# An MLP's other engines in a written order: ACT, DVE, POOL and SyncE follow the products' places

## The chip, the cores and the metric

The kernel runs on one core of one Trainium2 chip. It is one launch that computes a whole decoder block; the time is device microseconds of that launch. The core has five instruction streams that matter here: TensorE (PE, with the weight loads shown apart as PEld), VectorE (DVE), ScalarE (ACT), GpSimd (POOL) and SyncE (SP), which in the kernel before issues every DMA. Each stream runs its instructions in the order in which the built program has them and waits on semaphores for the others.

## The reference

The block has an attention and a gating branch, whose merged output is projected and added to x; the change leaves them alone. What matters is the squared-ReLU MLP behind them, on 2048 tokens, width 1024, inner width 4096, in float32:

```python
h = _rmsnorm(x, norm_pre_mlp[layer])
a = jax.nn.relu(jnp.einsum('bsd,df->bsf', h, w_mlp_in[layer]))
y = jnp.einsum('bsf,fd->bsd', a * a, w_mlp_out[layer])
x = x + _rmsnorm(y, norm_post_mlp[layer])
```

## The kernel before

**Numbers.** Each float32 operand is split in a high part (hi, rounded to the matmul's fp32r type: an ACT copy, L70) and a low part (lo, the difference: a subtraction on DVE or POOL, L75). A product of two operands is three matmuls: hi x hi, hi x lo, lo x hi.

**Products.** Both matrix products of the MLP use a scheme with seven block products in place of eight. Sums and differences of blocks are formed ahead, and the products are added up in PSUM and behind it.

GEMM1 (h times w_mlp_in) works on two token halves, first half 1 and then half 0, and in each on 16 pairs q of inner blocks. A product (L918) is 12 matmuls of 128x512. Names: A11, A12, A22, S1 to S4 are weight-side operands (tags wh and wl), B11, B21, B22 and T1 to T4 are token-side operands (T2_first is T2 of the first half). Digits behind a name are half and q: S2_13 is S2 of half 1, q = 3, and w1r_131 is the second raw weight tile of half 1, q = 3. For each q:

- two raw tiles w1r (512 KB each, tag w1r, 5 buffers) are loaded by SP; POOL forms four sums from them (L899 to L902, sum_a), ACT and DVE split the results;
- A11 and A12 of a q that stands in an "ahead" zone are loaded alone (lone_a, tile ar, 256 KB), in a buffer of the tag "c" that the outputs s1, s2, s4 use too;
- outputs: products 6 and 7 are added to xs on DVE (u6, u7, L939), products 5/7, 4 and 3 end in an add (L942) and relu and square on ACT (L927, L928); product 3 ends the q with four POOL operations (L955, L957, L959, L961). SP stores the seven results to sd in DRAM.

`places` sets PE's order by a place for each product: the first LEAD = 4 q have products 1 and 2 ahead, then a chain of five products per q, then seven products per q in the middle, and the last three q are again ahead and chain. The second half follows in the same way. The first products (A11, A12 with B11, B21) run while the block before, `out_block`, still transposes the last tokens; that block makes the T operands and stores them to td (L821), from which load_t fetches them.

GEMM2 has 64 steps (8 groups of two q, 8 token blocks), each with seven products of 6 matmuls (L1197). A step needs two tiles s (448 KB each from sd, split on ACT and DVE) and the split sums of w_mlp_out (B11y, T2y and so on, lo on POOL, sums by sum_w2 in tiles w2r). DVE adds each product to the accumulator (L1204, L1207 the first time). In the last group each finished row block goes through `finish`: square with a row sum on ACT (L1176), gain on POOL (L1177), rstd_of on DVE (L94 to L103), result on DVE (L1182), store.

**Order.** Only PE follows an order written out by hand, the order of the code. The other engines' instructions are put in order by the scheduler, which may move them past one another. In the built program DMAs signal through eight completion counters used in turn, so an issue can have to wait until the DMA eight issues earlier has landed.

```python
for z2 in order[n:n + 14]:
    raw_need(*z2)
for z2 in order[n:n + 6]:
    need(*z2)
product(*z)
```

So before, raw tiles are asked for 14 products ahead, and all five splits of a q at once, 6 products ahead.

## Time and profile before

| | us |
|---|---|
| median of 3 runs | 2871.11 (2864.7 to 2871.95) |
| the profiled execution, its own time | 2863.28 |
| its span, first to last instruction | 2861.5 |
| PE busy in it | 2729.3 |
| GEMM1, first product of q's chain to last product | 1537.0 to 2183.9 |
| GEMM2, first to last product | 2183.9 to about 2849.7 |

A row of a window gives, for each engine, its busy time in that stretch, with the number of instructions; then the granted clock of PE, the busy share of the DMA engines and GB/s. A row of waits gives who waits for whom, in total, how often, and the longest. A row of the timeline gives start, length, engine, line, operation, out<-in, and in brackets how long the engine stood idle before it and what released it. Rows of SPq are DMA issues: the length is that of the issue with its waiting. Rows of groups give count, busy time, mean ns of one, and idle time before them.

### The profile page before, as it was taken

The page shows a single profiled execution, that of the slowest core. Times are in us where ns is not written, and L with a number is a line of the kernel's source. Part 1 is how long each engine was busy: PE and PEld are TensorE (multiplying, and loading weights), DVE is VectorE, ACT ScalarE, POOL GpSimd, SP SyncE. Part 2 cuts the span into 40 slices and gives each one's busy share as a digit, 9 for nine tenths or more (in the row PEclk, how much of TensorE's full clock was granted, in tenths as well). Part 3 has the DMA queues.
Part 4 walks back from the last instruction along what each step waited for, and adds up shares of the span by engine and source line. Part 5 has one row for each costly group of instructions (what it writes and reads, how often), then busy time and mean ns, then how long its engine had stood idle before and what let it go on. Part 6 is the DMA issues. An engine that isn't in the chain of part 4 may idle for free. (4 is left out here: it accounts for less than half of the span.)

```text
span 2861.5 us, 36328 instructions
## 1 busy us (share of the span) xinstructions
PE 2729.3 (95%) x13364; PEld 2287.1 (80%) x13364; DVE 1587.3 (55%) x2684; ACT 1039.1 (36%) x2039; POOL 1003.7 (35%) x703
## 2 busy tenths in 40 slices
...
GB/s 252 176 150 149 173 135 180 142 201 177 203 210 199 163 199 128 204 171 183 143 186 234 155 158 159 191 174 157 157 156 209 117 95 125 126 120 125 127 137 196
DMA packets 348370, 475.38 MB, mean 166 GB/s; under 512 B 19872, under 2 KB 222880, under 8 KB 348192
## 3 DMA queue, kind: packets, MB, share of 16 engines
...
## 5 line engine op out<-in xcount | busy, mean ns | idle before, releaser
L70 ACT ACTIVATE s<-s 128x896 fp32r<-128x896 f32 x128 | 121.9, 953 | 269.8 <-PE ya L1197 137.8
L918 PE MATMUL aa<-B,A 128*128 128x512 f32 x768 | 191.2, 400 | 11.6 <-ACT A L70 9.3
L1204 DVE TENSOR_TENSOR acc<-acc,ya 128x512 f32<-128x512 f32 x224 | 151.4, 683 | 80.2 <-PE ya L1197 79.7
L75 DVE TENSOR_TENSOR s<-s 128x896 fp32r<-128x896 f32 x128 | 169.5, 1326 | 44.6 <-ACT s L70 44.4
L918 PEld LDWEIGHTS aa<-B,A 128*128 128x128 f32 x768 | 146.5, 192 | 47.5 <-ACT A L70 10.5
L72 POOL TENSOR_SCALAR w_g<-w_g_r 128x1024 fp32r<-128x1024 f32 x32 | 34.2, 1068 | 411.2 <-PE g L87 384.8
L85 PE MATMUL x<-hT_a,wq 128*128 128x512 f32 x384 | 149.7, 390 | 0.0
L87 PE MATMUL x<-hT_a,wq 128*128 128x512 f32 x384 | 149.4, 389 | 0.0
L86 PE MATMUL x<-hT_a,wq 128*128 128x512 f32 x384 | 149.4, 389 | 0.0
L603 DVE TENSOR_REDUCE o<-po 128x256 f32<-128x512 f32 x48 | 33.2, 691 | 183.9 <-PE po L602 183.9
L918 PE MATMUL ab<-T_first,S 128*128 128x512 f32 x384 | 96.7, 402 | 24.2 <-ACT T_first L70 15.9
L70 ACT ACTIVATE hl<-r 128x512 fp32r<-128x512 f32 x48 | 30.4, 633 | 231.5 <-POOL r L248 86.7
L1197 PE MATMUL ya<-T2y,s 128*128 128x512 f32 x384 | 100.0, 396 | 13.8 <-ACT s L70 13.8
L75 POOL TENSOR_TENSOR T2y<-w2r,T2y 128x512 fp32r<-128x512 f32 x16 | 20.5, 1306 | 262.4 <-ACT T2y L70 262.4
L1197 PE MATMUL ya<-B11y,s 128*128 128x512 f32 x384 | 103.0, 405 | 9.9 <-DVE acc L1204 9.9
L75 DVE TENSOR_TENSOR A<-w1r,A 128x512 fp32r<-128x512 f32 x68 | 64.8, 953 | 84.5 <-ACT A L70 84.4
L899 POOL TENSOR_TENSOR s<-w1r 128x512 f32<-128x512 f32 x32 | 43.8, 1369 | 191.6 <-DMA w1r<-in_w_mlp_in_dram 183.8
L1197 PE MATMUL yc<-B22y,s 128*128 128x512 f32 x384 | 100.8, 398 | 8.2 <-DVE acc L1204 8.2
L918 PEld LDWEIGHTS ab<-T_first,S 128*128 128x128 f32 x384 | 74.8, 196 | 41.5 <-ACT T_first L70 16.3
L755 POOL TENSOR_TENSOR g<-g,g 128x512 f32<-128x512 f32 x28 | 36.9, 1318 | 195.8 <-DVE v_pm L94 106.5
L85 PE MATMUL g<-hT_b,w_g 128*128 128x512 f32 x256 | 105.6, 412 | 0.0
L75 DVE TENSOR_TENSOR S<-w1r,S 128x512 fp32r<-128x512 f32 x96 | 95.5, 996 | 18.0 <-ACT S L70 17.0
...
## 6 DMA issues: line engine op xcount, KB each, us to landing
s<-sd SPq DMA_DIRECT2D x128, 448.0 KB, 3.8
w1r<-in_w_mlp_in_dram SPq DMA_DIRECT2D x64, 512.0 KB, 5.2
qk<-hl SPq DMA_DIRECT2D x24, 1024.0 KB, 5.3
...
w_g_r<-in_w_in_dram SPq DMA_DIRECT2D x32, 512.0 KB, 5.3
...
```

The lines of the kernel that those rows point to most:

```text
L70: act.activation(hi, src, AF.Copy)
L72: pool.tensor_scalar(hi, src, 1.0, 1.0, op0=OP.mult, op1=OP.mult)
L75: (pool if lo_eng == "pool" else dve).tensor_sub(lo, src, f32(hi))
L85: pe.matmul(ps, lh, rh, start=start, stop=False)
L86: pe.matmul(ps, lh, rl, start=False, stop=False)
L87: pe.matmul(ps, ll, rh, start=False, stop=stop)
L603: dve.tensor_reduce(ot[:, :, j * 64:(j + 1) * 64], po.rearrange("p (b h e) -> p b e h", b=4, h=2), axis=AX.X, op=OP.add)
L755: (dve if dt == KT - 1 else pool).tensor_add(parts[0], parts[0], parts[1])
L899: pool.tensor_add(s1, a21, a22)
L918: pe.matmul(p, w[:, l, k, :], h[:, r, k, :], start=i in (1, 6, 5) and not k and not n, stop=k == 3 and n == 2, skip_group_check=True)
L1197: pe.matmul(p, s[:, l], w[:, r], start=i in (1, 2, 5) and not m and not o, stop=m == 1 and o == 2, skip_group_check=True)
L1204: dve.tensor_add(an, an, p)
```

## The change

From the start of the MLP, ACT, DVE, POOL and SP too run in the order in which the code is written, and the code is written anew around the places of the products.

- LEAD is 5: five q ahead in each half. A raw lone tile is loaded by load_lone, up to nine places ahead and two at a time, on ACT's queue, into buffers of its own (tag ar); only those of q = 0 to 2 of the first half are loaded by SP, before the MLP, in buffers of the block before. T operands are loaded on ACT's queue as well, B11 and B21 on SP; splits stand some places behind the loads.
- w1r tiles are asked for 11 places ahead and only while a buffer is counted free; sums 6 places ahead; splits one product at a time, 4 places ahead with the product itself. Tag wh has 4 buffers (before 5), wl 6 (before 7).
- td is a DRAM tensor for each half; the x rows of every other block of the last chunk are loaded in a free part of `tail`.
- The first loads, splits and sums of GEMM2 (out_begin) are written between the last products of GEMM1. sum_w2 of a group is spread over two places.
- Splits of s stand apart from their loads, and their lo is done by POOL in the last group.
- In the last group square and gain are done for each quarter as it ends, the norm once per step for both row blocks (n = 2), and the four results one at each of the next products.

```diff
-    t_d = dtile([2, P, 5, 4, 512], "td")
+    t_d = [dtile([P, 5, 4, 512], f"td{h}") for h in range(2)]
...
-        xt = tp.tile([P, D], F32, name=f"xr_{c}{i}", tag="xr", bufs=1)
+        if c == chunks[3] and i % 2:
+            xt = tail[:, 40:].rearrange("p k c -> p (k c)")
+        else:
+            xt = tp.tile([P, D], F32, name=f"xr_{c}{i}", tag="xr", bufs=1)
...
+    early = {(1, q) for q in range(3)}
...
-    NQ, LEAD, TRAIL = NF // 2, 4, 3
-    b_, a_, araw, bank, xs_, u_, c1_ = {}, {}, {}, {}, {}, {}, {}
+    NQ, LEAD, TRAIL = NF // 2, 5, 3
...
-            split_in(w[:, :, k:k + 2], t_d[half][:, T_AT.index(name), k:k + 2], None, "act")
+            act.dma_start(f32(w)[:, 1, k:k + 2], t_d[half][:, T_AT.index(name), k:k + 2])
...
+    def alone(q):
+        return q < LEAD or q >= NQ - TRAIL
+    def load_lone(half, q, i):
+        if (half, q, i) not in lone_ and alone(q) and i < 3:
+            if (half, q) in early:
+                raw = gtp.tile([P, 512], F32, name=f"ar{i}_{half}{q}", tag=f"gt{i - 1}", bufs=2)
+            else:
+                raw = wp3.tile([P, 512], F32, name=f"ar{i}_{half}{q}", tag="ar", bufs=2)
             raw = raw.rearrange("p (k c) -> p k c", k=4)
+            (sp if (half, q) in early else act).dma_start(raw, a["w_mlp_in"][2 * q][:, i * 4 - 4:i * 4])
+            lone_[half, q, i] = raw
+    def load_a(half, q, i):
+        if alone(q) and i < 3:
+            return
+        raws = araw.setdefault((half, q), [])
+        free = 5 - sum(len(r) - ((*z, "A22") in a_) - ((*z, "S4") in a_) for z, r in araw.items())
+        for f in range(len(raws), min(2, len(raws) + free)):
             raw = wp3.tile([P, KT, P], F32, name=f"w1r_{half}{q}{f}", tag="w1r", bufs=5)
             sp.dma_start(raw, a["w_mlp_in"][2 * q + f])
-            araw[half, q].append(raw)
-    def sum_a(half, q):
+            raws.append(raw)
+    def sum_a(half, q, i):
+        if i < 3 or (half, q) in asum_:
+            return
         raw = araw[half, q]
         a11, a12, a21, a22 = (raw[f][:, k:k + 4] for f in range(2) for k in (0, 4))
-        names = ("S2", "S3", "S1", "A22", "S4")
-        w = {n: wp3.tile([P, 2, 4, P], F32R, name=f"{n}_{half}{q}", tag="wl", bufs=7) for n in names}
         s1 = wp3.tile([P, 4, P], F32, name=f"s1_{half}{q}", tag="s1", bufs=2)
-        t = dict(S1=s1, S3=a21, S2=a11, S4=a12, A22=a22)
+        asum_[half, q] = dict(S1=s1, S3=a21, S2=a11, S4=a12, A22=a22)
...
+    def split_a(half, q, i):
+        name = TERMS[i][0]
+        if (half, q, name) in a_:
+            return
+        if i < 3:
+            w = r3.tile([P, 2, 4, P], F32R, name=f"{name}_{half}{q}", tag="wh", bufs=4)
+            src = lone_[half, q, i] if alone(q) else araw[half, q][0][:, i * 4 - 4:i * 4]
+        else:
+            w = wp3.tile([P, 2, 4, P], F32R, name=f"{name}_{half}{q}", tag="wl", bufs=6)
+            src = asum_[half, q][name]
+        split(w[:, 0], w[:, 1], src)
+        a_[half, q, name] = w
...
+    def split_s(n, o):
+        g = ysteps[n][0]
+        w = st_[n, 2 * g + o]
+        split(w[:, 0], w[:, 1], f32(w)[:, 1], "act", "pool" if g == NQ // 2 - 1 else "dve")
...
+    def out_begin(n):
+        nonlocal r4
+        if n == 1:
+            er.close()
+            r4 = stack(e3, "r4", 1, side="right")
+            for q in range(2):
+                load_w2(q)
+            load_s(0)
+        elif n in (4, 5):
+            ops_of(0, n - 4)
+        elif n in (6, 7):
+            split_s(0, n - 6)
+        elif n in (8, 9):
+            sum_w2(n - 8)
...
+    in_order = ExitStack()
+    engines = {mybir.EngineType.Activation, mybir.EngineType.DVE, mybir.EngineType.Pool, mybir.EngineType.SP}
+    in_order.enter_context(tc.manual_schedule(engines=engines))
...
+    for n, name in enumerate(("T2", "T3", "T1", "T4", "B22")):
+        at(0 if n < 3 else 2, load_t, first_half, name, tt_[name])
+        at(2 + n, split_b, first_half, name)
+    for name in ("B11", "B21", "T2", "T3", "T1", "T4", "B22"):
+        n = ends[first_half, name]
+        at(n + 2, load_b if name in ("B11", "B21") else load_t, second_half, name)
+        at(n + 5, split_b, second_half, name)
+    n_out = max(ends[second_half, name] for name in ("B11", "B21"))
     for n, z in enumerate(order):
+        for z2 in order[n:n + 11]:
+            load_a(*z2)
+        for f, args in todo.pop(n, ()):
+            f(*args)
         for z2 in order[n:n + 6]:
-            need(*z2)
+            sum_a(*z2)
+        for _ in range(2):
+            for z2 in order[n:n + 9]:
+                if sum((h, q, TERMS[i][0]) not in a_ for h, q, i in lone_) < 2:
+                    load_lone(*z2)
+            for z2 in order[n:n + 4]:
+                if z2[2] > 2 or not alone(z2[1]) or z2 in lone_:
+                    split_a(*z2)
         product(*z)
...
+        if n > n_out:
+            out_begin(n - n_out)
...
+    def finish(n, ci, nh):
+        _, half, i = ysteps[n]
+        if n not in fs_:
+            fs_[n] = sm.tile([P, 2, 2], F32, name=f"fs_{n}", tag="fs")
+        y = acc[half, i, ci][:, nh * 512:(nh + 1) * 512]
+        junk = psum_any(f"jk_{n}{ci}{nh}")
+        act.activation(junk, y, AF.Square, accum_out=fs_[n][:, nh, ci:ci + 1])
+        pool.tensor_mul(y, y, gfin[nh])
+    def norm(n):
+        dve.tensor_add(fs_[n][:, 0], fs_[n][:, 0], fs_[n][:, 1])
+        fs_[n] = rstd_of(sm, fs_[n][:, 0], 2, 1.0 / D, f"fin{n}")
+    def result(n, ci, nh):
+        _, half, i = ysteps[n]
+        y = acc[half, i, ci][:, nh * 512:(nh + 1) * 512]
+        dve.scalar_tensor_tensor(y, y, fs_[n][:, ci:ci + 1], x1_[n, ci, nh], op0=OP.mult, op1=OP.add)
+        sp.dma_start(out[rows(half, i, ci), nh * 512:(nh + 1) * 512], y)
...
+            if i in (2, 5, 4, 3):
+                finish(n, ci, nh)
+            if i == 7:
+                load_x1(n)
+            if i == 3:
+                later.append((7 * n + 15, norm, (n,)))
+                later.extend((7 * n + 16 + m, result, (n, m // 2, m % 2)) for m in range(4))
...
+        if n + 1 < len(ysteps) and i in (1, 6):
+            split_s(n + 1, 0 if i == 1 else 1)
...
+            if place in (4, 5):
+                sum_w2(2 * g + place - 2)
```

Three places in the built programs. **ACT and SP at the start of GEMM1.** Before, SP issues the lone tiles, the raw tiles and the T loads; td is the store of the last tokens' T operands.

```order
L81 DMA ar0_13_13287<-in_w_mlp_in_dram 128x512
L924 DMA sd_82<-c11_10_13208 512x1x128
L81 DMA ar1_12_13312<-in_w_mlp_in_dram 128x512
L81 DMA ar1_13_13317<-in_w_mlp_in_dram 128x512
L924 DMA sd_82<-c11_11_13224 512x1x128
L888 DMA w1r_100_13274<-in_w_mlp_in_dram 128x1024
L821 DMA td_81<-tail_12725 2560x1x128
L888 DMA w1r_101_13276<-in_w_mlp_in_dram 128x1024
L888 DMA w1r_110_13278<-in_w_mlp_in_dram 128x1024
L81 DMA T2_first_13267<-td_81 128x1024 x2
```

After, these rows stand on ACT:

```order
L869 DMA T2_first_13278<-td1_82 128x1024 x2
L869 DMA T3_first_13277<-td1_82 128x1024 x2
L869 DMA T1_first_13276<-td1_82 128x1024 x2
L889 DMA ar1_13_13298<-in_w_mlp_in_dram 128x512
L889 DMA ar1_14_13300<-in_w_mlp_in_dram 128x512
L70 ACTIVATE A11_13_13302<-ar1_13_13298 128x512
L70 ACTIVATE A11_14_13305<-ar1_14_13300 128x512
L889 DMA ar2_13_13308<-in_w_mlp_in_dram 128x512
L889 DMA ar2_14_13310<-in_w_mlp_in_dram 128x512
L959 ACTIVATE xs_12_13325<-aa_12_13312 128x512
L70 ACTIVATE S2_10_13327<-w1r_100_13279 128x512
```

The loads of T2, T3 and T1 and of the lone tiles of q = 3 and 4 have moved to ACT, ahead of its splits, and the lone tiles stand behind the T loads.

**SP and DVE in the first half's chain.** sd stores are the outputs of q = 0. Before, on SP:

```order
L81 DMA B22_first_13263<-td_81 128x1024 x2
L888 DMA w1r_130_13426<-in_w_mlp_in_dram 128x1024
L888 DMA w1r_131_13428<-in_w_mlp_in_dram 128x1024
L924 DMA sd_82<-c11_13_13442 512x1x128
L888 DMA w1r_140_13528<-in_w_mlp_in_dram 128x1024
L924 DMA sd_82<-u7_10_13458 512x1x128
L924 DMA sd_82<-xs_10_13179 512x1x128
L924 DMA sd_82<-s1_10_13547 512x1x128
L924 DMA sd_82<-s2_10_13548 512x1x128
L888 DMA w1r_141_13530<-in_w_mlp_in_dram 128x1024
L924 DMA sd_82<-u6_10_13396 512x1x128
L924 DMA sd_82<-s4_10_13549 512x1x128
```

After, on SP and then on DVE:

```order
L901 DMA w1r_130_13508<-in_w_mlp_in_dram 128x1024
L951 DMA sd_83<-xs_10_13184 512x1x128
L951 DMA sd_83<-s1_10_13570 512x1x128
L951 DMA sd_83<-s2_10_13571 512x1x128
L951 DMA sd_83<-u6_10_13421 512x1x128
L951 DMA sd_83<-s4_10_13572 512x1x128
L901 DMA w1r_131_13598<-in_w_mlp_in_dram 128x1024
L951 DMA sd_83<-u7_11_13596 512x1x128
L901 DMA w1r_140_13620<-in_w_mlp_in_dram 128x1024
```

```order
L75 TENSOR_TENSOR S1_12_13645<-s1_12_13510,S1_12_13645 128x512
L969 TENSOR_TENSOR xs_11_13199<-xs_11_13199,ab_11_13518 128x512
L75 TENSOR_TENSOR S2_13_13664<-w1r_130_13508,S2_13_13664 128x512
L969 TENSOR_TENSOR u6_11_13531<-u6_11_13531,ac_11_13603 128x512
L75 TENSOR_TENSOR A22_12_13693<-w1r_121_13486,A22_12_13693 128x512
L966 TENSOR_TENSOR u7_12_13708<-xs_12_13325,ab_12_13630 128x512
L75 TENSOR_TENSOR S4_12_13712<-w1r_120_13394,S4_12_13712 128x512
```

w1r_131 has moved from ahead of all outputs of q = 0 to behind the last of them (s4_10); on DVE the lo of S2_13 stands ahead of the add that ends u6_11.

**POOL and SP at the end of GEMM1.** Before, on POOL (outputs s1 to s4 of q = 15, and the lo of T2y and T3y for GEMM2):

```order
L959 TENSOR_TENSOR u6_014_17879<-c11_014_17780,u6_014_17879 128x512
L961 TENSOR_TENSOR s4_014_18002<-xs_014_17644,s2_014_18001 128x512
L75 TENSOR_TENSOR T2y_0_18132<-w2r_0_18088,T2y_0_18132 128x512
L75 TENSOR_TENSOR T2y_1_18135<-w2r_1_18090,T2y_1_18135 128x512
L75 TENSOR_TENSOR T3y_0_18138<-w2r_0_18088,T3y_0_18138 128x512
L955 TENSOR_TENSOR s1_015_18073<-u6_015_17967,u7_015_18023 128x512
L75 TENSOR_TENSOR T3y_1_18141<-w2r_1_18090,T3y_1_18141 128x512
L957 TENSOR_TENSOR s2_015_18074<-s1_015_18073,c11_015_17811 128x512
L959 TENSOR_TENSOR u6_015_17967<-c11_015_17811,u6_015_17967 128x512
L961 TENSOR_TENSOR s4_015_18075<-xs_015_17720,s2_015_18074 128x512
```

After, on POOL (w2first4 is T2y of the first q) and then on SP:

```order
L1099 TENSOR_TENSOR w2r_1_17832<-w2r_1_17832 128x512
L1100 TENSOR_TENSOR w2r_1_17832<-w2r_1_17832 128x512
L982 TENSOR_TENSOR s1_014_18047<-u6_014_17881,u7_014_17958 128x512
L984 TENSOR_TENSOR s2_014_18048<-s1_014_18047,c11_014_17768 128x512
L986 TENSOR_TENSOR u6_014_17881<-c11_014_17768,u6_014_17881 128x512
L988 TENSOR_TENSOR s4_014_18049<-xs_014_17654,s2_014_18048 128x512
L982 TENSOR_TENSOR s1_015_18123<-u6_015_18000,u7_015_18073 128x512
L984 TENSOR_TENSOR s2_015_18124<-s1_015_18123,c11_015_17805 128x512
L986 TENSOR_TENSOR u6_015_18000<-c11_015_17805,u6_015_18000 128x512
L988 TENSOR_TENSOR s4_015_18125<-xs_015_17715,s2_015_18124 128x512
L75 TENSOR_TENSOR w2first4_18153<-w2r_0_17830,w2first4_18153 128x512
L75 TENSOR_TENSOR w2first5_18152<-w2r_1_17832,w2first5_18152 128x512
```

```order
L951 DMA sd_83<-s4_012_17737 512x1x128
L901 DMA w1r_0150_17746<-in_w_mlp_in_dram 128x1024
L951 DMA sd_83<-c11_014_17768 512x1x128
L951 DMA sd_83<-c11_015_17805 512x1x128
L1080 DMA w2r_0_17830<-in_w_mlp_out_dram 128x2x1024
L1080 DMA w2r_1_17832<-in_w_mlp_out_dram 128x2x1024
L1110 DMA s_00_17834<-sd_83 128x896
L1110 DMA s_01_17836<-sd_83 128x896
L901 DMA w1r_0151_17838<-in_w_mlp_in_dram 128x1024
L951 DMA sd_83<-u7_013_17824 512x1x128
```

T2y's lo now stands behind all outputs of q = 14 and 15, and the last raw tile, w1r_0151, behind the first loads of GEMM2.

203 lines of the change are left out of this document (81 added, 122 removed).

## The prediction

> **What bounds the kernel now.** I read the page's busy times first, then the list of what TensorE (PE) waits for, then windows over the MLP (from 1502 us to the end), and only then single engines at the places where PE stands still.
>
> ```profile
> PE 2729.3 (95%) x13364; PEld 2287.1 (80%) x13364; DVE 1587.3 (55%) x2684; ACT 1039.1 (36%) x2039; POOL 1003.7 (35%) x703
> ...
> 1640.00:1710.00 70.00, 70.00 (x309) 57.67 (x308) 34.10 (x44) 34.37 (x57) 42.74 (x30) 1.00 0.52 153
> 1780.00:1850.00 70.00, 63.49 (x269) 50.87 (x268) 35.76 (x39) 33.87 (x54) 35.12 (x24) 0.98 0.62 195
> 1850.00:1920.00 70.00, 58.05 (x221) 46.19 (x222) 40.87 (x44) 32.91 (x52) 31.05 (x20) 0.85 0.59 187
> 2800.00:2862.00 62.00, 41.16 (x150) 31.19 (x148) 53.07 (x112) 18.33 (x52) 25.24 (x19) 0.83 0.56 191
> ```
>
> The windows give PE, weight loads, DVE, ACT, POOL, then granted clock, DMA share and GB/s. In 1640 to 1710 PE never stops: 70.00 / 309 = 0.2265 us per matmul, so a product of GEMM1 (12 matmuls) takes 2.72 us and one of GEMM2 (6) about 1.4. PE is the bound, and the change touches neither its work nor its order before the MLP. Only its standing still can be won or lost:
>
> ```profile
> PE ab L918 <- DVE u L939: 16.3, 5, 4.4
> PE ab L918 <- ACT T_first L70: 15.9, 1, 15.9
> PE ya L1197 <- ACT s L70: 13.8, 1, 13.8
> PE ya L1197 <- DVE acc L1204: 12.6, 7, 2.7
> ...
> PE aa L918 <- ACT A L70: 9.3, 2, 5.5
> PE ab L918 <- DVE T_first L75: 5.2, 1, 5.2
> ...
> PE aa L918 <- DVE A L75: 2.0, 2, 1.6
> ```
>
> The start of GEMM1 is 15.9 + 5.2, the turn between its token halves 9.3 + 1.6 and part of the 16.3, the handover to GEMM2 13.8, the last group 12.6 and some. A stall costs more than its length, since the clock comes back slowly:
>
> ```profile
> 1605.75 5.46 PE L918 MATMUL ab<-T_first,A 128*128 128x512 f32 x12 [3.64 <-DVE u L939]
> ```
>
> Behind 3.64 us of waiting this product took 5.46 instead of 2.72: 2.7 us more.
>
> **Start of GEMM1.**
>
> ```profile
> 1513.89 1.04 PE L809 MATMUL pt<-ident,y 128*128 128x128 f32 x8
> ...
> 1537.04 0.80 PE L918 MATMUL ab<-T_first,S 128*128 128x512 f32 x1 [15.90 <-ACT T_first L70]
> ...
> 1561.05 2.94 PE L918 MATMUL ab<-T_first,A 128*128 128x512 f32 x12
> ...
> 1521.47 4.01 SPq L888 DMA_DIRECT2D w1r<-in_w_mlp_in_dram  x2
> ...
> 1529.88 1.26 POOL L899 TENSOR_TENSOR s<-w1r 128x512 f32<-128x512 f32 x1 [9.00 <-DMA w1r<-in_w_mlp_in_dram]
> ...
> w1r<-in_w_mlp_in_dram SPq DMA_DIRECT2D x9, 512.0 KB, 5.7
> T_first<-td SPq DMA_DIRECT2D x8, 512.0 KB, 7.4
> ```
>
> Eight products of A11/A12 are done by 1521.1 (1537.04 - 15.90); T2_first and the first w1r are late, since their issues stand behind the last store of td. With td in two tensors the T loads don't wait for that store, and they leave on ACT. Won, at most, are the 15.9. But with LEAD 5 the sixth product in PE's order is A11 of q = 3, and only q below 3 is loaded early. PE has five products, the last two behind the final transposes: 1514.9 + 2 x 2.72 = 1520.4 at the latest, some 2.5 sooner since the last x rows are loaded ahead. I take 1518. A11_13 is the seventh DMA issue in ACT's written row, behind two each of T2, T3 and T1. An issue that finds its completion counter taken blocks its engine: the two w1r issues above took 4.01 us where an issue is some 0.5. In the built program ACT's issues use counters that the last td store and the w1r loads behind it hold just then. Those land as the 1529.88 shows, so ar1_13 leaves at about 1531 and lands at 1535 to 1536; its split ends at 1536 to 1537. That is a stall of 18 us, then some 24 us of products at DVE's pace, until 13 products are done at about 1561.5; before it is 1561.05. I take 0. Bounds: all T and A in time, 15.9 won; ACT blocked one more DMA landing (5.7) with its clock loss, 10 lost.
>
> **The chains (five products per q).** In the written order of SP, w1r_131 stands behind s4_10, the last of four outputs that POOL makes for q = 0. POOL's sums of q = 3 need it, S2_13's lo follows them, and DVE's written row has that split ahead of the add on u6_11, which the outputs of q = 1 need. So from one q to the next runs a loop.
>
> ```profile
> L955 POOL TENSOR_TENSOR s<-u,u 128x512 f32<-128x512 f32 x4 | 5.6, 1402 | 3.4 <-ACT u L928 3.4
> L961 POOL TENSOR_TENSOR s<-xs,s 128x512 f32<-128x512 f32 x4 | 6.6, 1639 | 0.0
> L901 POOL TENSOR_TENSOR w1r<-s,w1r 128x512 f32<-128x512 f32 x5 | 7.1, 1423 | 0.4
> L75 DVE TENSOR_TENSOR S<-w1r,S 128x512 fp32r<-128x512 f32 x15 | 14.8, 984 | 0.4 <-ACT S L70 0.4
> L942 DVE TENSOR_TENSOR u<-u,ac 128x512 f32<-128x512 f32 x10 | 6.8, 681 | 2.9 <-PE ac L918 2.9
> L927 ACT ACTIVATE u<-u 128x512 f32<-128x512 f32 x10 | 6.3, 631 | 7.5 <-DVE u L942 7.2
> ...
> w1r<-in_w_mlp_in_dram SPq DMA_DIRECT2D x8, 512.0 KB, 4.8
> ```
>
> Its length: u6 add 0.68, relu and square 2 x 0.63, four outputs 5.6 to 6.6, issue 0.5 and load 4.8, three sums 3 x 1.42 = 4.3, hi 0.63 and lo 0.98: 18.8 to 19.8 us. PE spends 5 x 2.72 = 13.6 per q. S2_13 is used eight products (21.8 us) after the product that ends q = 0, so the first turn of the loop is hidden; each later one is 5 to 6 us too long, until 7 products per q (19.0 us) catch it. With LEAD 5 that is three turns in the first half, 16 us, and two in the second, 11 us. What the u waits and their clock cost there before is 6.5 and 7.5. Change: -10 - 3 = -13. Bounds: 0 (slack that the row order does not show) and -25 (the loop binds to the end of both chains).
>
> **Turn between the halves.**
>
> ```profile
> 1878.76 0.51 SPq L924 DMA_DIRECT2D sd<-s  x1
> ...
> 1880.54 0.40 SPq L81 DMA_DIRECT2D ar<-in_w_mlp_in_dram  x1
> ...
> 1885.87 0.63 ACT L70 ACTIVATE A<-ar 128x512 fp32r<-128x512 f32 x1 [0.64 <-DMA ar<-in_w_mlp_in_dram]
> ```
>
> The load of the lone A is issued behind stores that wait for POOL, into a buffer that it shares with these stores, and PE waits 5.46 for it. The windows 1780 to 1920 lack 40 + 88 of 309 matmuls, 29 us at 0.2265; with the waits of this stretch and their clock I count 26. After, the load has ACT's queue and buffers of its own and stands up to nine places ahead. What is left is about 3 us of u waits, so +23; the DMA share of 0.59 in 1850 to 1920 leaves the load room. Bounds: 9.3 + 1.6 = 11 (the A waits alone) and 26. The 46 issues that ACT gets, at 0.5, are 23 us over 600 in which it is busy by half (33 of 70): cover enough, except at the start.
>
> Here a page speaks against the change. The Trainium skill, "DMA: Bandwidth & Descriptors", section "Issuing engines are not separate DMA queues": DMAs of several issuing engines run on the same 16 DMA engines, and a second issuer saves only issue time. By it the turn gains nothing.
>
> **Handover to GEMM2.**
>
> ```profile
> 2193.46 6.32 DVE L75 TENSOR_TENSOR s<-s 128x896 fp32r<-128x896 f32 x3 [8.73 <-ACT s L70]
> ...
> 2184.75 2.56 POOL L75 TENSOR_TENSOR T2y<-w2r,T2y 128x512 fp32r<-128x512 f32 x2 [0.65 <-ACT T2y L70]
> ...
> w2r<-in_w_mlp_out_dram SPq DMA_DIRECT2D x2, 1024.0 KB, 7.4
> ```
>
> Now DVE does three s splits ahead of the accumulator copy that frees PE; T2y itself is ready in time. The new order takes the s splits early (13.8 and 2.4 of clock won). But w1r_0151 now stands on SP behind both w2r, whose room comes free only with the last use of B11/B21, 14 products (38.1 us) before GEMM1 ends; and 28 POOL operations stand ahead of T2y's lo from there (sums of q = 15, B11y and B21y, outputs of three q, sum_w2 twice). With loads of 8 to 12 us, 28 x 1.28 (half the 2.56 above) to 1.64 and T2y's own 1.3 it is ready 45 to 59 us on, where PE wants it at 38.1 + 2.8 = 41. Lost 4 to 18 and 2.4; in the middle 13.5. I take 16, nearer the contended POOL rows: 0 won, bounds -4 and +9.
>
> **Last group and tail.**
>
> ```profile
> L1177 POOL TENSOR_TENSOR acc<-acc,gfin 128x512 f32<-128x512 f32 x29 | 39.2, 1372 | 50.3 <-ACT jk L1176 50.3
> L1182 DVE SCALAR_TENSOR_TENSOR acc<-acc,r_fin,x 128x512 f32<-128x512 f32 x32 | 26.5, 861 | 0.4
> L75 DVE TENSOR_TENSOR s<-s 128x896 fp32r<-128x896 f32 x10 | 12.0, 1203 | 0.0
> L103 DVE TENSOR_TENSOR r_fin<-r_fin,t_fin 128x1 f32<-128x1 f32 x16 | 7.9, 496 | 0.1
> L94 DVE TENSOR_SCALAR v_fin<-fs 128x1 f32<-128x1 f32 x15 | 2.2, 146 | 0.2
> ...
> 2774.17 1.61 PE L1197 MATMUL ya<-B11y,s 128*128 128x512 f32 x6 [1.55 <-DVE acc L1204]
> ...
> 2827.55 2.90 PE L1197 MATMUL ya<-B11y,s 128*128 128x512 f32 x6 [2.75 <-DVE acc L1204]
> ```
>
> Four steps take 53.4 us, 13.35 each against 7 x 1.4 = 9.8. DVE per step: seven adds of 0.68 (4.8), four results (3.4), two norms of three operations at up to 0.50 and three at 0.15 (3.7), two s splits (2.4): about 14, the bound. The change takes the splits off and makes one norm of four and three (2.4): 10.6. POOL gets them: 4 x 1.37 + 2 x 1.37 x 896/512 = 10.3. Two-operand DVE work waits for a busy POOL: L103 against L94, 0.35 us at a POOL share of 25.24 / 62 = 0.41. With twice the share, eight such operations a step wait 0.35 more each: 13.4. The adds with one operand in PSUM show no such wait. I take 12.9, half a microsecond won on each of six steps, +3; bounds 10.6 (+16) and 14.4 (-6). After the last product DVE has one norm and no split in its way, and four results: +2, between 0 and 4. The other groups of GEMM2: 0.
>
> The Trainium skill, "SBUF — State Buffer", section "Who interferes with whom", makes it an exclusive lock: a two-input DVE instruction and a GpSimd instruction that reads SBUF block each other for a whole instruction. By it the wait doubles with POOL's share, and the last group gains next to nothing.
>
> **Sum.** 0 - 13 + 23 + 0 + 3 + 2 = 15 us off the profiled execution's 2863.3: 2848. The median of the runs is 2871.1, 7.8 above it; the new median may lie as far above its own lowest, so I say 2851.
>
> **Rivals.** (a) The loops don't bind: the chain rows hide slack, T and A come in time, DVE's step falls to its sum. Then 13 (start), 23, 10 (handover and tail), 9 (last group) are won: about 2808. For it: PE's 7-product zone runs without a gap at these very POOL loads. Against it: w1r_131 really stands behind s4_10. 0.20. (b) Slower: one mechanism, the loop of the chains, longer and without the hidden first turn (w1r buffers that come free late would do that). With the load at the start's 5.7 and outputs and sums at 6.6 and 4.5 a turn takes 20.9 us, 7.3 over PE's 13.6. Four turns in each half lose 58, which is 44 more than the 14 there before; the turn and the end still win 28: 2863 + 44 - 28 = 2879. It decides from 5.3 us over PE's time in all eight turns, where the loss passes 28. For it: SP's and DVE's rows close the loop in each q. Against it: two w1r buffers are free at first. 0.17. (c) The change doesn't do what it says: the lone A at the turn still comes late, since the DMA engines or the counters hold it, and +23 goes: 2871. 0.18. The Trainium skill, by the section on issuing engines named above, would have this one.
>
> **How the numbers follow.** Forecast 0.45, its own range 2835 to 2866. The 8 in 10 reach into both sides: 2815 to 2877. A measurement can't tell 0.3% (8.6 us) from none: faster is below 2862.5, from the forecast 0.39, (a) 0.20, (c) 0.02, 0.61 in all; within, 0.06 + 0.13 = 0.19; slower 0.17 + 0.03 = 0.20.
>
> **What would show it.** The start: one PE wait of 15 to 20 us on A (ACT) with A11_13, and 13 products done near 1561. The chains: waits ab on S (DVE or ACT) growing from the second q, w1r issues behind s4 stores. The turn: no aa wait over 2 us. The handover: a ya wait on T2y by POOL. The last group: DVE no longer 14 of a step, L103 longer than 0.50, steps near 13. Wrong it is if the chains run without gaps or PE still waits for a lone A at the turn.

## The result, and the profile after

The change makes the kernel slower: a median of 2919.36 us (2913.71 to 2921.65, 4 runs) against 2868.5 for the kernel before on the same chip (2864.7 to 2871.95), a ratio of 1.0175 [1.0152, 1.0197]. The forecast was 2851, with 8 in 10 between 2815 and 2877; it gave a slower kernel a chance of 0.20, and its dearest rival ended at 2879. The profiled execution took 2917.28 us with a span of 2915.5, 54.0 over the span before.

The page of the changed kernel, busy times and the queues:

```profile
PE 2754.8 (94%) x13364; PEld 2298.5 (79%) x13364; DVE 1568.2 (54%) x2628; ACT 1022.3 (35%) x2031; POOL 1022.3 (35%) x719
...
q10 hardware_dynamic: 6912, 18.22, 1.9%
```

TensorE does the same 13364 matmuls; it is busy 25.5 us longer with them, at a mean granted clock of 0.971 against 0.977, and the rest of the 54 is standing still. q10 is ScalarE's new queue: 18.22 MB. What TensorE waits for (engine, line, releaser: us in total, times, longest):

```profile
PE aa L945 <- ACT A L70: 26.1, 2, 24.5
PE ya L1258 <- POOL s L75: 16.8, 7, 3.0
PE ab L945 <- DVE u L966: 15.5, 8, 3.3
PE ab L945 <- ACT S L70: 12.2, 7, 4.5
PE b L85 <- DVE g L753: 11.2, 5, 4.1
PE ya L1258 <- ACT s L70: 9.4, 7, 2.0
PE pt L812 <- DVE y L803: 9.3, 6, 4.0
PE ya L1258 <- DVE s L75: 6.1, 8, 0.9
PE pv L596 <- ACT ph L582: 5.4, 2, 3.3
PE ya L1258 <- POOL w2first L75: 5.0, 1, 5.0
```

The waits of before on T_first (15.9 + 5.2), on s at the handover (13.8) and on the accumulators (12.6 + 8.2, now 1.4) are gone. In their place stand one long wait on a lone A, and many short ones on u, S and s.

A table by stage says more than the list. The MLP has 672 products in one fixed order, 224 in GEMM1 and 448 in GEMM2. Each figure is the time from the start of one product to the start of another in TensorE's timeline, in us. "Full speed" is the number of products times the 2.72 (GEMM1) of the prediction. The four kernels to the right are experiments, told of below.

| products | stage | full speed | before | after | c3 | c6 | c8 | c10 |
|---|---|---|---|---|---|---|---|---|
| ahead of 0 | all that comes first | | 1502.2 | 1510.9 | 1506.3 | 1509.3 | 1506.4 | 1510.7 |
| 0-13 | start of GEMM1 | 35.4 | 61.7 | 65.8 | 57.1 | 54.2 | 56.5 | 56.5 |
| 13-33 | first chain | 54.4 | 61.2 | 64.0 | 68.1 | 60.6 | 60.6 | 57.5 |
| 96-123 | turn | 73.4 | 102.0 | 97.3 | 96.9 | 98.3 | 98.9 | 88.2 |
| 123-150 | second chain | 73.4 | 80.6 | 84.9 | 82.6 | 73.9 | 73.9 | 73.6 |
| 216-224 | end of GEMM1 | 21.8 | 23.0 | 39.2 | 40.1 | 33.4 | 33.5 | 24.9 |
| 224-234 | handover | | 30.2 | 24.6 | 24.2 | 24.5 | 22.5 | 33.2 |
| 234-608 | seven groups of GEMM2 | | 522.8 | 545.0 | 517.1 | 517.1 | 517.1 | 517.2 |
| 608-640 | last group, first part | | 50.7 | 56.0 | 49.1 | 49.3 | 48.2 | 49.1 |
| 640-671 | last group, rest | | 59.8 | 60.4 | 57.5 | 57.5 | 58.6 | 57.6 |
| | span | | 2861.5 | 2915.5 | 2866.4 | 2846.9 | 2845.1 | 2835.7 |

The stretches left out (33-96, 150-216) agree within 0.5 us. After against before: 8.7 us are lost ahead of the MLP; 4.2 at the start; 2.8 and 4.3 in the chains; 16.2 at GEMM1's end; 22.2 in the seven groups; 5.9 in the last. Won are 4.7 in the turn and 5.6 in the handover. The sum is the 54.

Two of these need care. Of the 8.7, 5.2 are there at 1392.85, ahead of anything that the change touches, and at that place the traces of this document lie anywhere from 1389.3 to 1398.0, whatever their edit. The other 3.5 are not chance: from TensorE's matmul at 1470.0 to the MLP's first product it is 32.2 us before (31.7 in b6, an edit of the kernel before), 35.7 after, and 34.6 to 37.5 in every other kernel with the written order. And 65.8 is short for the start of the changed kernel: e1, e2, e5, e10 and e13 leave the start as it is and take 67.7 to 68.6 there.

### The profile page after: what moved, and what is told of

The parts are those of the page before. It is cut to its first block, busy times and chain, and to the rows that moved or that the text cites. A ratio compares the mean times of both kernels' runs of the same rounds, so it can differ in the third digit from the quotient of the medians.

```text
span 2915.5 us, 36261 instructions
## 1 busy us (share of the span) xinstructions
PE 2754.8 (94%) x13364; PEld 2298.5 (79%) x13364; DVE 1568.2 (54%) x2628; ACT 1022.3 (35%) x2031; POOL 1022.3 (35%) x719
## 3 DMA queue, kind: packets, MB, share of 16 engines
q10 hardware_dynamic: 6912, 18.22, 1.9%
## 5 line engine op out<-in xcount | busy, mean ns | idle before, releaser
L75 DVE TENSOR_TENSOR s<-s 128x896 fp32r<-128x896 f32 x112 | 150.1, 1340 | 118.0 <-ACT s L70 118.0
L603 DVE TENSOR_REDUCE o<-po 128x256 f32<-128x512 f32 x48 | 33.2, 691 | 184.5 <-PE po L602 184.5
L1258 PE MATMUL ya<-B11y,s 128*128 128x512 f32 x336 | 95.3, 409 | 30.5 <-POOL s L75 16.8
L945 PE MATMUL ab<-T,S 128*128 128x512 f32 x384 | 101.3, 414 | 14.4 <-ACT S L70 8.8
L1258 PEld LDWEIGHTS ya<-B11y,s 128*128 128x128 f32 x336 | 63.9, 192 | 53.2 <-POOL s L75 19.8
L85 PE MATMUL g<-hT_a,w_g 128*128 128x512 f32 x256 | 104.8, 410 | 0.0
L85 PE MATMUL o<-wo,mg 128*128 128x512 f32 x256 | 102.5, 400 | 1.5 <-ACT mg L70 0.8
L945 PEld LDWEIGHTS ab<-T,S 128*128 128x128 f32 x384 | 75.8, 200 | 34.8 <-ACT S L70 10.4
L1265 DVE TENSOR_TENSOR acc<-acc,yc 128x512 f32<-128x512 f32 x128 | 87.5, 683 | 27.8 <-PE yc L1258 22.4
```

Source lines behind the costliest of these rows:

```text
L75: (pool if lo_eng == "pool" else dve).tensor_sub(lo, src, f32(hi))
L85: pe.matmul(ps, lh, rh, start=start, stop=False)
L603: dve.tensor_reduce(ot[:, :, j * 64:(j + 1) * 64], po.rearrange("p (b h e) -> p b e h", b=4, h=2), axis=AX.X, op=OP.add)
L945: pe.matmul(p, w[:, l, k, :], h[:, r, k, :], start=i in (1, 6, 5) and not k and not n, stop=k == 3 and n == 2, skip_group_check=True)
L1258: pe.matmul(p, s[:, l], w[:, r], start=i in (1, 2, 5) and not m and not o, stop=m == 1 and o == 2, skip_group_check=True)
L1265: dve.tensor_add(an, an, p)
```

## The experiments

Each ratio is to the kernel before, with its 95% interval. The ten e kernels differ from the changed kernel by one edit each (e11 by two); c3 and c4 join several; b6 is an edit of the kernel before; c8 to c11 are built on c6.

**The seven groups: e1.** ScalarE's rows in the third step of a group, and below them SyncE's queue:

```profile
2325.62 0.95 ACT L70 ACTIVATE s<-s 128x896 fp32r<-128x896 f32 x1 [8.64 <-DMA s<-sd]
2329.21 0.63 ACT L70 ACTIVATE B11y<-w2r 128x512 fp32r<-128x512 f32 x1 [2.63 <-DMA w2r<-in_w_mlp_out_dram]
2331.70 0.63 ACT L70 ACTIVATE B11y<-w2r 128x512 fp32r<-128x512 f32 x1 [1.86 <-DMA w2r<-in_w_mlp_out_dram]
2332.24 0.93 ACT L70 ACTIVATE s<-s 128x896 fp32r<-128x896 f32 x1
```

```profile
2301.76 20.33 SPq L1110 DMA_DIRECT2D s<-sd  x6
2322.20 2.35 SPq L1080 DMA_DIRECT2D w2r<-in_w_mlp_out_dram  x2
```

The loads of the next group's w2 stand behind loads of s that wait for a buffer (for TensorE's products on the s before, by the queue's own list); they leave at 2322.2, and one step later ScalarE waits for them with B11y's hi, and the split of s that TensorE needs next stands behind it in the written order.

```diff
-            if place in (2, 3):
-                ops_of(g + 1, place - 2)
-            if place in (4, 5):
-                sum_w2(2 * g + place - 2)
+            if place in (3, 4):
+                ops_of(g + 1, place - 3)
+            if place in (5, 6):
+                sum_w2(2 * g + place - 3)
```

> In GEMM2 the splits of the next group's B11y, B21y and the sums of w2 stand one step later in the written order (places 3, 4 and 5, 6 in place of 2, 3 and 4, 5); nothing else. Theory A: ACT's written row has B11y's hi, which waits for the load of w2r, ahead of the second s split, and PE waits for that split once per group (2.7 + 1.1 + 0.5 = 4.3 us in each of seven groups). Then these stalls go: PE's waits on s by ACT and DVE (9.4 and 6.1 us) fall under 3 together, and GEMM2's seven groups get 22 to 30 us shorter; total about 2890. Theory B (rival): the s tile itself lands late because the two 1 MB loads of w2r share the DMA engines with it. Then the stall stays where it is, within 1 us per group, and the total within 8 us of the 2917 of the changed kernel.

Measured: 2883.97, ratio 1.0044 [1.0021, 1.0067], span 2882.3: 33 us less. Of these, 27.9 lie in the seven groups; 4.7 lie ahead of the MLP, where this edit does nothing. A group falls from about 81.5 to 77.4 us per 56 products, less than the 78 of before, and TensorE no longer waits in it. This one wait was the largest single part of the loss, and the prediction had a 0 there.

**GEMM1's end, first try: e2.** The work of `out_begin` is one product later.

```diff
-            out_begin(n - n_out)
+            out_begin(n - n_out - 1)
```

> All first loads, splits and sums of GEMM2 that are written between GEMM1's last products stand one product later, so that the last raw tile w1r_0151 is loaded ahead of both w2r and the first s, not behind them. Theory A: POOL's sums of q = 15 waited 13.9 us for that tile, because its load shared the engines with 3 MB issued just before it; with it goes the stall on S2_15 (4.6 and 3.4 us) and what follows from it in the last six products, 16.4 us in all: GEMM1 ends 10 to 16 us earlier against its own middle. The handover to GEMM2 then costs the same or up to 5 more, since POOL's row ends no earlier than its sum. Total 2903 to 2910. Theory B (rival): POOL's row of 28 operations is the limit at this end, whichever load comes first; then what is won on S2_15 comes back as a wait on T2y, and the total stays within 4 us of 2917.

2905.79, ratio 1.0119 [1.0089, 1.0148]. The wait on S2 of q = 15 (4.5) is gone, but products 216 to 224 fall only from 39.2 to 35.0: waits on u stay (8.2). The raw tile that came late was worth 4 of the 16 us that the stage loses. The total is where theory A had it, but 6.7 us of that lie ahead of the MLP, where this edit does nothing.

**The start: e3, e6, e11.** ScalarE's rows, and TensorE's wait:

```profile
1526.08 19.08 ACTq L869 DMA_DIRECT2D T_first<-td  x6
1545.19 2.50 ACTq L889 DMA_DIRECT2D ar<-in_w_mlp_in_dram  x2
1551.96 1.25 ACT L70 ACTIVATE A<-ar 128x512 fp32r<-128x512 f32 x2 [25.26 <-DMA ar<-in_w_mlp_in_dram]
```

```profile
1552.64 3.78 PE L945 MATMUL aa<-B,A 128*128 128x512 f32 x8 [24.52 <-ACT A L70]
```

Six issues hold ScalarE for 19.08 us, where an issue that waits for nothing takes 0.33 to 0.5 in this trace. e3 puts the first three T behind the lone loads; e6 takes the T one after the other; e11 is e6 with td's last store ahead of the first products.

```diff
 e3
-        at(0 if n < 3 else 2, load_t, first_half, name, tt_[name])
+        at(1 if n < 3 else 2, load_t, first_half, name, tt_[name])
 e6, e11
+        at((1, 3, 4, 5, 6)[n], load_t, first_half, name, tt_[name])
+        at((2, 5, 6, 7, 8)[n], split_b, first_half, name)
 e11 alone, behind the first load_lone
+    store()
```

> At the start of GEMM1 the six T loads on ACT's queue are issued one product later, behind the lone loads of q = 3 and 4 and behind the splits of A11_13 and A11_14. Theory A: ACT stood 19.1 us in these six issues (1526.1 to 1545.2), each waiting for a completion counter, and ar1_13 behind them was late for that alone: now it is issued at about 1526, PE's wait of 24.5 us on A11_13 falls to 4 to 8, and the wait moves to T2 or S2_10; 13 products are done 10 to 17 us earlier; total 2900 to 2907. Theory B (rival): the load itself is slow, since the last store of td and four w1r tiles hold the DMA engines until 1540; then the wait on A11_13 stays over 15 us and the total within 5 us of 2917.

> As the kernel with the T loads behind the lone loads, but only T2 is loaded there; T3 and T1 are issued three and four products on, T4 and B22 five and six, and their splits later too. Theory A: once the lone tiles are early, the start is bound by bytes: in the 28 us from the first td store on, the DMA engines moved 310 to 430 GB/s without a gap and a w1r tile took 10.0 us in place of 5.7, because 2 MB of T3 and T1 and 2.6 MB of td went with them. With T3 and T1 out of the way w1r_101 lands 5 to 8 us earlier, POOL's sums of q = 0 start at about 33 us after the MLP's first product in place of 38.8, and 13 products are done 55 to 60 us after it (63.9 with the T loads only one product later, 65.8 to 68.4 in the changed kernel). Total 2900 to 2906. Theory B (rival): the w1r issues on SP wait for completion counters that the td stores hold, whatever else is loaded; then the sums start within 2 us of 38.8 and the 13 products take 62 to 66.

> As the kernel with T2 alone behind the lone loads, and the td store of the third token block stands on SP ahead of the first two sd stores, not behind them with the last td store. Theory A: SP stood 7.3 us in the sd stores of c11_10 and c11_11, which wait for PE's products, with a td store behind them that had long been ready; then two td stores went out together, took 12.2 us to land (6.9 for one in the kernel before) and held the engines and the counters when the w1r tiles followed. With one of them gone ahead POOL's sums of q = 0 start 28 to 33 us after the MLP's first product (37.4 in that kernel, 27.7 in the kernel before) and 13 products are done in 51 to 56 us (60.6 there, 61.7 before). Theory B (rival): the last td store alone, with ar and T2 beside it, fills the engines until the tiles come; then the sums start within 2 us of 37.4 and the 13 products take 59 to 61.

e3: 2912.01, ratio 1.014 [1.0111, 1.017]. The six T issues, now behind the lone loads, still hold ScalarE 15.83 us. The wait on A falls to 2.0, and 13.7 and 1.2 appear on T2 (ScalarE's hi, VectorE's lo): the stage is 63.9. On ScalarE the hi of T2 stands behind that of S2 of q = 0 (1548.20), and S2 needs GpSimd's sums (to 1548.16), which start late:

```profile
1544.23 1.26 POOL L915 TENSOR_TENSOR s<-w1r 128x512 f32<-128x512 f32 x1 [21.62 <-DMA w1r<-in_w_mlp_in_dram]
```

That is 38.8 us behind the first product, against 27.7 before. e6: 2909.75, 1.0143 [1.0101, 1.0185]; the sums start at 37.4 and the stage takes 60.6, between its two theories. e11: 2906.11, 1.0118 [1.0097, 1.0139]; the sums start 33.1 behind the first product, and the stage takes 56.6, 9 less than in the changed kernel and 5 less than before. So the start has two limits in series: issues that block ScalarE, and behind them the td store and load and the raw tiles, which share the DMA engines. That they share them is read from the traces; no run shows it apart. And in e6 and e11 the first chain is 68.6 and 67.5 in place of 64.0: of what the start wins, 4.6 of 5.2 and 3.5 of 9.2 us are lost at once in the chain.

**The chains: e7, e13, b6.** e7 splits left operands three products ahead in place of four, so that the lo rows stand behind more of VectorE's additions. e13 has six raw tiles (w1r) and five split ones (wl) in place of five and six, the same bytes. b6 does that to the kernel before.

```diff
 e7
-            for z2 in order[n:n + 4]:
+            for z2 in order[n:n + 3]:
 e13
-        free = 5 - sum(
+        free = 6 - sum(
-            ... tag="w1r", bufs=5)
+            ... tag="w1r", bufs=6)
-            ... tag="wl", bufs=6)
+            ... tag="wl", bufs=5)
 b6, on the kernel before
-            ... tag="w1r", bufs=5)
+            ... tag="w1r", bufs=6)
-        ... tag="wl", bufs=7) for n in names}
+        ... tag="wl", bufs=6) for n in names}
```

> Operands of GEMM1 are split three places ahead in place of four (with the product itself), so S2's lo of the q after next stands behind the add that ends u6 on DVE, not ahead of it; nothing else. Theory A (the loop of the prediction): the two chains lose 9.6 us (products 13 to 33) and 9 to 11 us (123 to 150) because u6's add waits for S2's lo, which waits for POOL's sums, the w1r tile and the outputs of the q before. With the add ahead of it the loop is cut, and each chain loses at most 5; total 2903 to 2909. Theory B (rival): the w1r tile simply comes late, since its buffer is freed late by the splits; then splitting later frees it later still, the chains lose as much or more (9 to 15 each), and the total is 2915 to 2930.

> Six buffers for raw tiles w1r in place of five, five for split operands (tag wl) in place of six, since the memory doesn't hold more; nothing else. Theory A: in the chains w1r_131 and its like are late because no buffer is free until the splits of q = 0 are written, so that they stand behind the s4 store; with a sixth buffer they stand a place or two earlier, ahead of it, and the chains lose at most 5 us each (products 13 to 33: at most 59 us, 64.0 now; 123 to 150: at most 79, 82 to 85 now). Total 2906 to 2912. Theory B (rival): POOL's and DVE's rows set the chain, not the tile; then both stretches stay within 1.5 us, or get longer by the waits for one split buffer fewer.

> The kernel before with nothing changed but the buffers of GEMM1's left operands: six raw tiles (w1r) in place of five, and six split ones (wl) in place of seven, the same bytes. The kernel before loses 6.8 us in products 13 to 33 (61.2 against 54.4 without a wait) and 7.2 us in products 123 to 150 (80.6 against 73.4). Theory A, that the sixth raw tile is all that these chains want, in whichever order the engines are written: both come to within 1 us of 54.4 and 73.4, and the kernel is 12 to 14 us faster (ratio 0.995). Rival B, that the order of before holds them by something else (the smaller number of split tiles, or the place of the loads on SyncE): the two stages stay within 2 us of 61 and 81, and the time within 4 us of before.

e7: 2926.95, 1.0203 [1.0153, 1.0252]. The chains get no shorter (63.5 and 82.4), the zone of seven products per q, which ran without a gap, loses 5.7 and 7.2, and the turn 9.5. Lo rows ahead of the additions are not what closes the loop. GEMM1's end does get shorter (31.0 in place of 39.2); what did that was not taken apart.

e13: 2893.12, 1.0073 [1.0051, 1.0094]. The two chains take 54.40 and 73.92, full speed to half a microsecond. The waits of the changed kernel in the first chain, which the next fence lists, are all gone in e13:

```profile
PE ab L945 <- ACT S L70: 3.0, 2, 2.8
PE ab L945 <- DVE u L966: 2.3, 2, 2.0
PE ab L945 <- DVE S L75: 1.0, 2, 0.5
```

b6: 2859.49, ratio 0.9959 [0.9944, 0.9974]. The second chain falls from 80.6 to 74.0; the first only to 59.8, the start is 2 longer, and the handover 4.4. So the sixth raw tile is what the second chain wants under either order. Of the first chain that holds only in e13, behind a slow start (68.6). One reading is that start and first chain wait for the same loads (0 to 33 together: before 122.9, b6 123.5, e13 123.0, c3 125.3); it is not shown, and c6 and c10 (114.8 and 114.0, below) stay under that sum.

**The queues: e4, e10.** e4 gives all of ScalarE's loads of T and lone A to SyncE; e10 gives the lone tiles three buffers and lets three be on their way.

```diff
 e4
-            act.dma_start(f32(w)[:, 1, k:k + 2], t_d[half]...
+            sp.dma_start(f32(w)[:, 1, k:k + 2], t_d[half]...
-            (sp if (half, q) in early else act).dma_start(raw, ...
+            sp.dma_start(raw, ...
 e10
-            ... tag="ar", bufs=2)
+            ... tag="ar", bufs=3)
-                if sum(...) < 2:
+                if sum(...) < 3:
```

> All loads are issued by SP again, in the written order; ACT issues none but one s load. Theory A: a second issuing engine helps only where SP waits with something else ahead: at the turn the lone tiles now stand behind stores that wait for POOL, and 96 to 123 takes 100 to 106 us (97.3 with ACT's queue, 102.0 in the kernel before); at the start ACT is no longer blocked in T issues, but the T loads stand behind four w1r tiles and two td stores, so 13 products take 60 to 70 us as now. Total 2915 to 2925. Theory B (rival, by the Trainium skill, DMA: Bandwidth & Descriptors, section Issuing engines are not separate DMA queues): the same 16 engines carry the loads in either case, an issue costs 0.5 us, and no stage moves by more than 2 us.

> Three buffers, not two, for the late lone tiles (tag ar), and up to three of them unsplit at a time. Theory A: at the turn the lone tiles run in a loop of their own: a load of 4.3 to 5.7 us, hi on ACT, lo on DVE, and only then the next load into the same buffer, which with two buffers gives one A per 3.5 us or so, while PE wants ten among 15 products. With three buffers the products 96 to 123 take 90 to 94 us in place of 97.3 (73.4 is the sum of the products); total 2910 to 2914. Theory B (rival): the A tiles wait in ACT's and DVE's written rows behind T and B splits and u adds, not for their buffers; then 96 to 123 stays within 2 us of 97.3.

e4: 2917.29, 1.0169 [1.0099, 1.0239], span 2908.3. The start takes 68.4, as in the kernels that leave it as it is (67.7 to 68.6), the turn is 2.3 shorter, where theory A had it longer, and no other stage is longer by more than 1.5: the second queue itself wins nothing. By the Trainium skill, "DMA: Bandwidth & Descriptors", section "Issuing engines are not separate DMA queues", a second issuer saves issue time alone; the trace agrees with that. e10: 2915.62, 1.0163 [1.0116, 1.021], turn 97.7 against 97.3: the buffers of the lone tiles don't hold it.

**The last group: e5.** The lo rows of s go back to VectorE.

```diff
-        split(..., "act", "pool" if g == NQ // 2 - 1 else "dve")
+        split(..., "act", "dve")
```

> In the last group the lo of the s splits is done by DVE again, as in the kernel before; the norm for two rows at once and the results one by one stay. Theory A: POOL's row (four gains and two lo's, each waiting for the other operations of its row and held up by DVE's two-operand work) sets the 13.6 us of a step; with the lo's on DVE its sum is 10.6 + 2.4 = 13.0 and POOL is free, so a step takes 12 to 13 us, the waits on POOL's s (16.8 us) go, and the last group gets 4 to 10 us shorter; total 2907 to 2913. Theory B (rival): DVE is the limit in either case, as in the kernel before; then a step takes 13.4 to 14.5 us and the total is the same or higher by up to 5.

2905.82, 1.0119 [1.0089, 1.0148]. Products 608 to 640 take 48.2 in place of 56.0, less than the 50.7 of before, and 640 to 671 take 58.6. In the changed kernel TensorE waited there for GpSimd's lo rows, seven times in all (16.8), and from 2780 to 2848 four times:

```profile
PE ya L1258 <- POOL s L75: 10.2, 4, 3.0
```

**Several together: c3, c4, c6.** c3 is e1, e2, e5, e11 and three buffers for the lone tiles, with splits three ahead behind the last use of B11 and B21; c4 has the second half's lone tiles on SyncE and neither e2 nor the third buffer; c6 is e1, e2, e5, e11 and e13.

> Together: w2 operands one step later in GEMM2; GEMM2's first loads one product later; s lo on DVE in the last group; T2 alone behind the lone loads; td store early; three buffers for the lone tiles, still two unsplit at a time; from the last use of B21 on, splits three places ahead. If the parts add up: the changed kernel's 2917 less 33 (groups), 10 (last group), 8 to 12 (end of GEMM1 and handover), 7 to 12 (start), 2 (turn): 2848 to 2860, a ratio to the kernel before of 0.992 to 0.997. If they take each other's gains (a stage's end only moves the wait on), 2865 to 2880.

> As c3, but GEMM2's first loads stand where the change put them, and the lone tiles of the second half are loaded by SP with two buffers, not by ACT with three. If ACT's queue costs what the kernel with all loads on SP showed (products 96 to 123 in 95.0 us in place of 97.3), that stretch takes 94 to 96; if the early w2 loads cost only their 4 us, the end of GEMM1 (216 to 234) takes 57 to 62 here and 3 to 5 less in c3. Total 2850 to 2865.

> The changed kernel with the places of GEMM2's right operands one step later (as e1), out_begin one place later (as e2), the last group's lo rows on VectorE (as e5), the stores of td ahead of the first products and the T operands one after the other (as e11), and six raw tiles (as e13). Theory A, that the gains of the single runs add: against c3 (span 2866.4), which has all but the raw tiles, products 13 to 33 fall from 68.1 to 54 or 56, products 123 to 150 from 82.6 to 74, and the end of GEMM1 (216 to 224) from 40 to 35: 25 us less, some 2842 us, ratio 0.990. Rival B, that what the raw tiles held is held next by the bytes of the start (c3's start of 57.1 us was short because its first chain took what the loads still lacked): products 0 to 33 stay over 118 us (c3: 125.3) and the time is 2852 to 2858.

c3: 2867.67 (10 runs), 0.9987 [0.9978, 0.9997]. c4: 2865.05 (10 runs), 0.9984 [0.9971, 0.9998]. So with all the losses mended that had been found by then, the written order comes to no more than level with the kernel before; the first chain (68.1) has swallowed the start's gain. c4 misses its own expectations by stage: the turn takes 96.7, and the end with the handover 71.3, of which the handover has 36.4. Its profiled execution took 2876.12, at the upper end of its ten runs. c6: 2849.71, 0.9933 [0.9918, 0.9949]: with the sixth raw tile the second chain is at full speed, the first at 60.6. The gains add but for these 6 us, and the time lies between the two that were expected.

**GEMM1's end again: c8, c9, c10.** c8 is c6 with the split of s for GEMM2's first step behind GEMM1's last product. c9 is c8 with three lo rows of w2first on VectorE. c10 is c8 with ScalarE's squares written behind the next step's splits.

```diff
 c8
-        elif n in (6, 7):
-            split_s(0, n - 6)
+    for o in range(2):
+        split_s(0, o)
     ea.close()
 c9
-    split(w[:, 0], w[:, 1], raw, "act", "pool")
+    split(w[:, 0], w[:, 1], raw, "act",
+          "dve" if 5 <= n_op[0] <= 10 and q % 2 else "pool")
 c10
             dve.tensor_add(t, t, p)
-            square(t, t)
+            late_.append(lambda: square(t, t))   # stores, POOL's sums too
...
+        squares()          # runs what is in late_
         product(*z)
```

> The kernel of c6 with the two splits of s for GEMM2's first step (two rows of 0.9 us on ScalarE, two of 1.6 to 1.8 us on VectorE) moved behind GEMM1's last product; the loads, the first four right operands of w2 and the sums on GpSimd stay among the last eight products. Theory A, that it is these rows, ahead of the evictions and the splits that the last products wait for, which lengthen GEMM1's end: products 216 to 224 are 4 us or more shorter than in c6, and the handover (224 to 234) is longer by 3 at most: 2 to 5 us less in all. Rival B, that GEMM1's end is held by the loop of eviction on VectorE, square on ScalarE and split behind it in the written order: 216 to 224 shorten by under 2 us, the handover is 2 to 4 longer, the time the same or longer.

> The kernel of c8 with the lo rows of three of GEMM2's ten late first operands (w2first) on VectorE in place of GpSimd, whose ten rows take 15.1 us in one piece behind GEMM1. Theory A, that the handover's wait is on GpSimd's row of lo: the handover (224 to 234, 24.2 to 24.7 us with 14 without a wait) is 3 to 4 us shorter than in c8. Rival B, that the two engines run slower side by side (VectorE's rows of lo took 1.7 to 2.2 us there against 0.7 to 1.2 alone) or that s or the left operands' hi on ScalarE is late next: within 1 us of c8.

> The kernel of c8 with one thing written otherwise in GEMM1's products: ScalarE's two rows of relu and square on a product's result (with the stores and GpSimd's sums behind them) stand behind the splits of the next step in place of ahead of them. In c8's last eight products the chain of waits goes round once a product: VectorE's eviction (ends 2169.1) > ScalarE's squares (2169.08 to 2170.37) > its hi of S (2170.28) > VectorE's lo of S (2170.92 to 2172.26) > the next eviction, which frees the bank (2172.87) > TensorE (2173.01). Theory A, that this circle through two written orders holds GEMM1's end: it is broken by the new place, and products 216 to 224 take 22 to 26 us in place of 33.5 (21.8 without a wait), the kernel 6 to 10 us less. Rival B, that GpSimd's sums of w1r (4 of 1.3 to 1.7 us ahead of each S) hold it: the stage stays over 31 us. The turn (96 to 123, 98.9) has the same circle in places but waits for other things there: 0 to 5 us less by A.

c8: 2846.9, 0.992 [0.9907, 0.9934]. The end stays at 33.5: there its rival was right, though the handover is 2 shorter, not longer. c9: 2845.72, 0.992 [0.9906, 0.9933], the handover 23.1: again the rival. c8's trace shows a circle; VectorE, ScalarE and TensorE in one turn of it:

```profile
2168.37 0.68 DVE L969 TENSOR_TENSOR u<-u,ac 128x512 f32<-128x512 f32 x1
2170.92 1.34 DVE L75 TENSOR_TENSOR S<-w1r,S 128x512 fp32r<-128x512 f32 x1 [1.88 <-ACT S L70]
2172.19 0.68 DVE L966 TENSOR_TENSOR u<-xs,ab 128x512 f32<-128x512 f32 x1
```

```profile
2169.08 0.63 ACT L954 ACTIVATE u<-u 128x512 f32<-128x512 f32 x1 [2.50 <-DVE u L969]
2169.74 0.63 ACT L955 ACTIVATE u<-u 128x512 f32<-128x512 f32 x1
2170.28 0.61 ACT L70 ACTIVATE S<-w1r 128x512 fp32r<-128x512 f32 x1
```

```profile
2166.02 2.88 PE L945 MATMUL ac<-T,S 128*128 128x512 f32 x12
2173.01 1.56 PE L945 MATMUL ab<-T,A 128*128 128x512 f32 x3 [4.10 <-DVE u L966]
```

VectorE adds to u; ScalarE squares it; only then, by its written order, comes S's hi, whose data had been there long before (GpSimd's last sum of w1r ends at 2146.33); VectorE's lo of S waits for the hi; and the addition that frees TensorE's bank stands behind that lo. From one addition of L969 to the next (2164.06, 2168.37, 2172.97) it goes round in 4.3 and 4.6 us, where a product takes 2.72.

c10: 2835.82, 0.9867 [0.9852, 0.9881]. The end falls from 33.5 to 24.9, the turn from 98.9 to 88.2, the first chain from 60.6 to 57.5. At the end theory A holds: the rows above close the circle between ScalarE and VectorE alone. For the turn the gain is twice what was expected, and there a second circle is at work, for the edit moves not only the squares but the stores and GpSimd's output sums too. At the start of the turn in c8, GpSimd stands 9.80 us for a square with the next sums of w1r written behind that output, the loads of B stand on SyncE behind the stores, and ScalarE stands 7.53 us for a sum (rows of GpSimd, SyncE and ScalarE):

```profile
1795.80 1.29 POOL L982 TENSOR_TENSOR s<-u,u 128x512 f32<-128x512 f32 x1 [9.80 <-ACT u L955]
1803.59 0.89 SPq L860 DMA_DIRECT2D B<-h2d  x2
1805.78 0.63 ACT L70 ACTIVATE S<-w1r 128x512 fp32r<-128x512 f32 x1 [7.53 <-POOL w1r L917]
```

In c10 sums and loads come first:

```profile
1790.22 1.29 POOL L915 TENSOR_TENSOR s<-w1r 128x512 f32<-128x512 f32 x1 [2.16 <-DMA w1r<-in_w_mlp_in_dram]
1792.16 0.91 SPq L860 DMA_DIRECT2D B<-h2d  x2
```

The changed kernel has the same two waits at that place (9.79 and 7.54). How much of the 10.7 us each order is worth is not told apart, since no run moves the squares alone.

But c10's handover grows from 22.5 to 33.2, and with the end it is 58.0 us against c8's 56.0: here the gain is all given back. TensorE's longest wait in it, the row of VectorE that ends it, and what GpSimd does meanwhile:

```profile
2184.98 1.65 PE L1271 MATMUL ya<-B11y,s 128*128 128x512 f32 x3 [7.95 <-DVE s L75]
```

```profile
2175.79 9.13 DVE L75 TENSOR_TENSOR s<-s 128x896 fp32r<-128x896 f32 x1 [6.24 <-ACT s L70]
2171.56 12.42 POOL L75 TENSOR_TENSOR w2first<-w2r,w2first 128x512 fp32r<-128x512 f32 x10
```

This lo row of s has its operands at 2175.76, and a row of its form takes 1.07 or 1.08 us in c10 a little later; here it takes 9.13 and ends 0.95 us after the last of GpSimd's ten rows. The same row takes 9.03 in c11, 8.89 in c4 and 8.46 in b6, and these four are the kernels whose handover takes 33 us or more; in all the others no such row in the handover takes over 2.3, and the two engines' rows take turns. So most of what c10 gives back is VectorE held up beside a full run of rows on GpSimd. That is read from the traces of four kernels; no run moves GpSimd's rows in c10, and c9, which moves three of them, starts from c8, where VectorE isn't held like this.

**The turn: c11.** c8's turn begins with this wait of TensorE, and with these rows of VectorE ahead of the addition that it waits for:

```profile
1816.69 1.62 PE L945 MATMUL ab<-T_first,A 128*128 128x512 f32 x3 [6.40 <-DVE u L966]
```

```profile
1810.85 3.44 DVE L75 TENSOR_TENSOR B<-B 128x1024 fp32r<-128x1024 f32 x2 [3.17 <-ACT B L70]
1814.20 1.75 DVE L75 TENSOR_TENSOR A<-w1r,A 128x512 fp32r<-128x512 f32 x1
1815.87 0.68 DVE L966 TENSOR_TENSOR u<-xs,ab 128x512 f32<-128x512 f32 x1
```

c11 is c10 with the splits of the second half's B11 and B21 three products later.

```diff
-        at(n + 5, split_b, second_half, name)
+        at(n + (8 if name in ("B11", "B21") else 5), split_b, second_half, name)
```

> The kernel of c10 with the splits of the second half's B11 and B21 written eight products behind their last use in the first half in place of five (their loads stay two behind it). In c8 TensorE stands 6.4 us at the product that starts at 1816.69, for the eviction u of VectorE at 1815.87, which stands behind the lo of B (1810.85 to 1814.29), behind ScalarE's hi of B, which waited for the load until 1809.76. Theory A, that this one wait is the start of the turn: the wait of 6.4 us goes, and the turn (96 to 123) is 4 to 7 us shorter than in c10. Rival B, that what is saved there is lost at the second half's first products, whose operands come from the same two engines: the stretch from 96 to 104 is shorter, 104 to 123 longer by as much, the turn within 2 us of c10.

2835.09, 0.9871 [0.9855, 0.9888]: no different from c10. That wait of 6.40 is already down to 0.26 in c10, where the loads of B leave at 1792.16, not 1803.59, and the turn is 88.4 against 88.2. The turn still takes 15 us more than full speed; TensorE's longest waits left in it are 3.8 on VectorE's lo of an S and 3.5 on a lone A, and what holds these was not taken apart.

b6 and c10 both have the sixth raw tile. Each was measured against the kernel before (0.9959 and 0.9867), so the change with these repairs is worth some 0.9% beside the kernel before with the same tile.

## Why the prediction was wrong

The sign was wrong. Three terms of the sum carry the miss: the other groups of GEMM2, put at 0, lost 22.2 us; the turn, put at +23, won 4.7; the handover with GEMM1's end, put at 0, lost 10.6. What they have in common is that the prediction followed single waits and not what stands behind a waiting row on the same engine. Taken by its own steps:

- **Ahead of the MLP:** not in the sum. 8.7 us later in the profiled execution: 5.2 of them differ from one execution to the next, 3.5 are in the last rows of `out_block`, as in every kernel with the written order. What makes these 3.5 was not looked into.
- **Start, forecast 0** (stall 18, 13 products done some 59 us after the first): the mechanism was right, blocked issues on ScalarE ahead of the lone A. It was undersized: the lone load left at 1545.2, not 1531 (34.3 us behind the first product, not 28.8), the stall was 24.5, and 4.2 us were lost, within the bound of 10. Two slips in that part: eight products were said to be done by 1521.1 before, where TensorE's order has six, since the seventh is an S; and 1561.05 is the start of the thirteenth product, so that thirteen are done at 1563.8.
- **Chains, -13, bounds 0 to -25:** measured -7.1. The loop of store, load, sum and split is real as far as its link through the raw tile goes: a sixth tile breaks it (e13). The loss after the change was put at 16 and 11 and is 9.6 and 11.5: the first half's was too large. The prediction put what the kernel before loses there (6.8 and 7.2) down to waits on u; b6 shows that in the second chain it is the same shortage of a raw tile. The step from addition to split in the loop is not borne out (e7).
- **Turn, +23, bounds 11 to 26:** measured +4.7, outside the bounds. The step that failed is "what is left is about 3 us of u waits". The waits on the lone A fall from 10.9 to 3.1, as said, but TensorE still waits 14.7 in all: 4.5 on u, 4.2 on S and 2.9 on ScalarE's xs besides. It stands in circles that the written order closes, with squares, stores and output sums ahead of the next operands: writing these later takes 10.7 off the turn (c8 to c10). Rival (c) came near for this stage with the wrong cause: the lone A is the smaller part of the waits, and neither a third buffer (e10) nor the queue (e4) changes the stage by more than 2.4.
- **Handover, 0, bounds -4 to +9:** measured -10.6 with GEMM1's end (53.2 to 63.8), outside the bounds. The wait on w2first was 5.0, where 16 was put on T2y. The loss lies ahead of it, among the last eight products, where the prediction looked at GpSimd's 28 operations alone and not at the row order of ScalarE and VectorE (c8 to c10: 8.6 us).
- **Last group, +3, bounds -6 to +16:** measured -5.3 from 608 to 640 and -0.6 behind. The rows were sized about right: a lo row takes 2.14 us on GpSimd (median of 15), where the sum had 2.4, and 1.27 on VectorE in e5 (median of 16). The step that failed is that the group was priced by each engine's total: behind GpSimd's products with gfin the lo row comes too late, and TensorE waited 16.8 us for it. e5 shows that the kernel is better without this move. The Trainium skill, "SBUF — State Buffer", section "Who interferes with whom", would have given next to nothing, nearer than +3; the wait that the trace shows is another, on GpSimd's rows themselves, and no run here takes the lock apart from them.
- **Tail, +2:** from the start of the last product to the end it is 14.2 us before and 14.4 after: nothing.
- **Other groups of GEMM2, 0:** measured -22.2, the largest single miss. It was costed at nothing without a row being named that hides it. ScalarE's order puts B11y's hi, which waits for w2, ahead of the split of s, and SyncE's order puts w2 behind loads that wait for buffers; both could be read from the written order (e1).
- **The sum:** 2848 with 7.8 on top would be 2856, not 2851; that is small beside the miss.

Against the 54 us stand 27.9 that e1 takes off in the seven groups (which end below the level of before), 9.6 by e5, 9 by e11 at the start, of which the first chain takes 3.5 back, and the circles, which cost 8.6 at the end of GEMM1 in c8 (given back in the handover once they are open) and 10.7 in the turn, where before had losses of its own.
